# In the last group of a trunk layer's channel mixer, two more up channels by seven products, in turns with a pair; the group's weight sums on VectorE; one plain tile's low part by transfer

## The chip, the cores and the metric

One core of one Trainium2 chip runs the whole layer in one launch. The metric is the device time of one execution in microseconds (us). The kernel before has a median of 824.56 us of 3 runs (824.37 to 825.36). Engines: TensorE (PE, with its weight loads as PEld), VectorE (DVE), ScalarE (ACT), GpSimd (POOL), and SyncE (SP), which issues most loads.

## The reference

A decoder layer on 512 tokens of 1024 channels, all in float32. The part that matters here is the channel mixer at its end:

```python
u2 = _rmsnorm(h, norm2_g[l])
z = _causal_dwconv(u2 @ w_ffn_up[l], ffn_dw_w[l], ffn_dw_b[l])
h = h + (jax.nn.silu(z[..., :FFN_DIM]) * z[..., FFN_DIM:]) @ w_ffn_down[l]
```

`w_ffn_up` is 1024 x 5632, `w_ffn_down` 2816 x 1024, and the depthwise convolution has three taps. 2816 channels are 22 tiles of 128: "channel i" below means the value tile i and its gate tile 22 + i, two tiles of the up projection with 512 tokens each.

## The kernel before, in words

**Products.** TensorE multiplies in a rounded float32 form, so each weight and each activation is held as a high and a low part: ScalarE casts the high part, VectorE subtracts it from the original to get the low part, and each product is three matmuls (`mm3`, lines 448 to 450: high x low, low x high, high x high). A plain tile (`col_tile`) is 8 rows of 128 inputs x 3 matmuls of 512 columns. A weight tile of 128 x 1024 is loaded by SyncE into one of four `raw` buffers, then split (`split_weight`) into `whi` and `wlo`, four buffers each. `weight` hands out the next weight of a fixed list (`order`) and splits up to two ahead (`LOOK`). For some tiles (`ADDED`) the low part isn't VectorE's: ScalarE writes the negated rounded weight into `wlo`, and an accumulating transfer from GpSimd's queue adds the original from memory (lines 387 and 388).

**By seven.** A pair of tiles can be computed with Strassen and Winograd's seven products instead of eight: inputs halved (k), tokens halved (256), the two tiles being the output halves. `two_tiles` does so for channel i in four parts, named after the weight sums that they use: x1 (two products, 24 matmuls of 256 columns), x3 (24), x2 (24) and x4 (12). It uses three PSUM banks x, y, z, and two SBUF tiles c1 and c2 for the combined halves: ScalarE copies a bank's half out (line 1180), VectorE combines (line 1183). The sums of activations that the products need are made once, in the first group. The weight sums are made per channel on GpSimd (`two_sums`, line 327): from the two raw tiles "one" and "two" a third raw tile is filled, four additions of 128 x 512 per channel.

**Groups and units.** The 22 channels go in three groups of pairs (`GROUPS`; the last is (12, 14), (13, 15), (16, 18), (17, 19)). After each group the down projection of its pairs runs, also by seven products (`seven`), and adds to the residual `hres`. Within a group `up_plan` writes out the order: a *unit* is the second channel q of one pair by seven, in turns with the first channel f of the next pair as two plain tiles in pieces. In the last group the units are (14 with 13), (15 with 16), (18 with 17), and at the end channel 19 plain. The first unit starts with a piece of a plain tile ("opens"), and in every unit a piece of a plain tile stands between x2 and x4 of the pair.

**After a channel.** `value` and `gated` run the three taps: ScalarE the first with the bias (line 1499), VectorE two (line 1502) for each of the two tiles; then silu on ScalarE and the product on VectorE (line 1516). `first_of_pair` and `second_of_pair` make the sums for the down projection and split them (lines 1522 to 1544). `third_ahead` splits an x3 part one weight further ahead; the second channel's work is issued behind that low part and behind the last tap (`third`).

**Queues.** Each engine has one queue in order, and the order is settled when the program is built. VectorE's queue in the last group holds low parts (lines 356 and 390), combines, taps and the pair's sums; SyncE's the raw loads; GpSimd's the weight sums and then the accumulating transfers for the down projection (lines 300 and 317).

```python
seq = [x1, a1, x3, a2, x2, b1, x4, ("second", q), b2]
return seq + [("first", f)]
```

## Time and profile before

| | |
|---|---|
| median of 3 runs | 824.56 us (824.37 to 825.36) |
| the profiled execution | 825.34 us |
| its span, first to last instruction | 823.6 us |
| granted TensorE clock, mean | 0.999 |
| weight sums on GpSimd, L327 | 56 in the whole kernel, 12 of them from 700 to 750 us |
| last group, up projection | about 704.5 to 779 us |
| last group, down projection | about 779 to 814 us |

How to read it: the profile is of one execution. Busy time is the time that an engine had an instruction running; matmuls overlap, so TensorE's durations (0.28 us for 256 columns, 0.39 for 512) are longer than the distance from one start to the next, and that distance is the cost. The chain that ended last is followed back from the last instruction to what released it. A row of the view in order of time has the start in us from the span's begin, the duration, the engine, the line, the operation, the tiles written and read, the shape, how many in a row, and in brackets the idle time ahead with its releaser.

### The profile page before, as it was taken

Reading aid. Unit: us, or ns where it says so; the run is one execution under the profiler, and the core shown is the slowest. Engines: PE = TensorE matmul, PEld = TensorE weight load, DVE = VectorE, ACT = ScalarE, POOL = GpSimd, SP = SyncE. Lnnn points to the kernel's source line nnn. Section 1 sums busy time; section 2 is a strip of 40 time slices with the busy share of each in tenths; the row PEclk is TensorE's granted clock in tenths of the full one; section 3 lists DMA queues with packets and bytes.
Section 4 is the critical chain, followed back from the end, with each engine's and each line's share of the span. In section 5 each row is a group of like instructions: output and inputs, shape, how many; then the busy total and the mean of one; then the engine's idle time right before and its main releaser. Section 6 shows DMA issues by size and latency. Waiting matters only on the chain.

```text
span 823.6 us, 11562 instructions
## 1 busy us (share of the span) xinstructions
PE 814.8 (99%) x4323; PEld 703.4 (85%) x4323; DVE 719.2 (87%) x1165; ACT 450.0 (55%) x666; POOL 148.7 (18%) x133
## 2 busy tenths in 40 slices
PE   9999999999999999999999999999999999999996
PEld 7888888888888889999988898898889988899885
DVE  6689999998989699886788789979975999789996
ACT  6643447656654456684454546556435653456654
POOL 2000010001010213443001100230123301522012
PEclk9999999999999999999999999999999999999999
DMA  8355572553433103323647623145632456334662
GB/s 316 98 124 148 147 187 99 129 154 103 96 109 103 51 27 121 110 78 110 210 112 213 178 98 103 31 170 158 142 131 89 139 141 164 105 103 142 190 129 103
DMA packets 30616, 106.27 MB, mean 129 GB/s; under 512 B 3464, under 2 KB 3600, under 8 KB 30560
## 3 DMA queue, kind: packets, MB, share of 16 engines
q1 hardware_dynamic: 24784, 85.34, 30.3%
q0 software_dynamic: 5760, 20.19, 14.3%
q8 instruction: 34, 0.56, 0.3%
q14 instruction: 22, 0.18, 0.1%
q10 hardware_dynamic: 16, 0.00, 0.0%
HBM read 103.42 MB, written 2.10 MB: 128 GB/s over the span
## 4 chain that ended last, share of the span: by engine, by line
PE 98%; ACT 1%; DVE 0%; issue 0%; POOL 0%; POOLq 0%; ACTq 0%
PE mm L448 28%; PE mm L449 28%; PE mm L450 28%; PE mm L662 2%; PE ax L449 2%; PE ax L450 2%; PE ax L448 2%; PE ax L1069 1%; PE ax L1071 1%; PE ax L1050 1%; PE ax L1037 1%; PE mm L568 0%; PE ax L576 0%; PE ax L529 0%; PE ax L1035 0%; PE ax L1084 0%
## 5 line engine op out<-in xcount | busy, mean ns | idle before, releaser
L448 PE MATMUL mm<-uh,wlo 128*128 128x512 f32 (+1 forms) x672 | 244.5, 364 | 0.0
L449 PE MATMUL mm<-ul,whi 128*128 128x512 f32 (+1 forms) x672 | 242.3, 361 | 0.0
L450 PE MATMUL mm<-uh,whi 128*128 128x512 f32 (+1 forms) x672 | 242.1, 360 | 0.0
L450 PEld LDWEIGHTS mm<-uh,whi 128*128 128x128 f32 x672 | 126.8, 189 | 19.5
L448 PEld LDWEIGHTS mm<-uh,wlo 128*128 128x128 f32 x672 | 127.0, 189 | 18.8
L449 PEld LDWEIGHTS mm<-ul,whi 128*128 128x128 f32 x672 | 127.0, 189 | 18.6
L385 ACT CAST whi<-raw 128x1024 fp32r<-128x1024 f32 x86 | 89.5, 1046 | 58.2 <-PE mm L450 29.8
L356 DVE TENSOR_TENSOR wlo<-raw,whi 128x1024 fp32r<-128x1024 f32 x80 | 93.1, 1171 | 25.3 <-ACT whi L355 21.3
L327 POOL TENSOR_TENSOR raw<-raw,raw 128x512 f32<-128x512 f32 x42 | 67.5, 1608 | 212.3 <-DVE wlo L356 107.1
L390 DVE TENSOR_TENSOR wlo<-raw,whi 128x1024 fp32r<-128x1024 f32 x70 | 92.2, 1320 | 13.4 <-ACT whi L385 13.4
L355 ACT CAST whi<-raw 128x1024 fp32r<-128x1024 f32 x80 | 76.3, 957 | 36.1 <-PE mm L450 28.3
L788 DVE SCALAR_TENSOR_TENSOR c<-h,pp,c 128x255 f32<-128x255 f32 (+14 forms) x120 | 56.0, 467 | 3.2 <-ACT c L784 3.1
L788 DVE SCALAR_TENSOR_TENSOR c<-aside,btmp,c 128x255 f32<-128x255 f32 (+14 forms) x120 | 56.1, 467 | 0.0
L788 DVE SCALAR_TENSOR_TENSOR aside<-h,pp,aside 128x255 f32<-128x255 f32 (+6 forms) x112 | 52.3, 467 | 0.0
L355 ACT CAST whi<-kept 128x1024 fp32r<-128x1024 f32 (+1 forms) x32 | 31.7, 995 | 32.0 <-DVE kept L310 15.7
L1502 DVE SCALAR_TENSOR_TENSOR tmp<-mm,pp,tmp 128x511 f32<-128x511 f32 (+1 forms) x56 | 41.3, 740 | 4.0 <-ACT tmp L1499 3.9
L356 DVE TENSOR_TENSOR wlo<-kept,whi 128x1024 fp32r<-128x1024 f32 (+1 forms) x32 | 36.9, 1152 | 4.9 <-ACT whi L355 4.8
L1180 ACT COPY tmp<-mm 128x256 f32<-128x256 f32 x48 | 17.6, 367 | 33.8 <-PE mm L450 33.3
L1418 DVE TENSOR_TENSOR hres<-hres,mm 128x512 f32<-128x512 f32 (+1 forms) x49 | 32.2, 668 | 2.6 <-PE mm L450 2.4
L1499 ACT ACTIVATE tmp<-mm,pp 128x512 f32<-128x512 f32 x28 | 21.8, 777 | 19.1 <-PE mm L450 18.9
L387 ACT ACTIVATE wlo<-raw 128x1024 fp32r<-128x1024 f32 x16 | 16.9, 1059 | 22.1 <-PE mm L448 22.1
L1502 DVE SCALAR_TENSOR_TENSOR tmp<-tmp,pp,tmp 128x511 f32<-128x511 f32 (+1 forms) x32 | 27.7, 886 | 0.4
(351 smaller groups left out, 1777.5 us busy)
## 6 DMA issues: line engine op xcount, KB each, us to landing
raw<-in_w_up_dram SPq DMA_DIRECT2D x44, 512.0 KB, 4.2
raw<-in_w_glu_dram SPq DMA_DIRECT2D x16, 512.0 KB, 5.2
raw<-in_w_down_dram SPq DMA_DIRECT2D x15, 512.0 KB, 4.2
kept<-in_w_down_dram POOLq DMA_DIRECT2D x10, 512.0 KB, 5.7
raw<-in_w_v_dram SPq DMA_DIRECT2D x8, 512.0 KB, 5.8
raw<-in_w_qk_dram SPq DMA_DIRECT2D x8, 512.0 KB, 3.4
raw<-in_w_r_dram SPq DMA_DIRECT2D x8, 512.0 KB, 4.5
wlo<-in_w_r_dram POOLq DMA_DIRECT2D x8, 512.0 KB, 8.0
```

What stands on the lines that cost most here:

```text
L327: work = nc.gpsimd.tensor_tensor(out, x, y, ALU.add)
L355: nc.scalar.copy(hi, raw)
L356: two_low[:] = [nc.vector.tensor_tensor(lo, raw, hi.bitcast(F32), ALU.subtract)]
L385: nc.scalar.copy(hi, raw)
L390: pace[0] = nc.vector.tensor_tensor(lo, raw, hi.bitcast(F32), ALU.subtract)
L448: nc.tensor.matmul(acc, ll, rh, start=first, stop=False, **kw)
L449: nc.tensor.matmul(acc, lh, rl, start=False, stop=False, **kw)
L450: nc.tensor.matmul(acc, lh, rh, start=False, stop=last, **kw)
L788: nc.vector.scalar_tensor_tensor(out[:, j:], x[:, : half_t - j], w, out[:, j:], ALU.mult, ALU.add)
L1418: done = nc.vector.tensor_tensor(hres[t, n][:, c], hres[t, n][:, c], acc[:, c], op)
L1499: nc.scalar.activation(z, acc, AF.Identity, bias=pp[:, PP_FB + m : PP_FB + m + 1], scale=w[2])
L1502: nc.vector.scalar_tensor_tensor(z[:, s:], acc[:, : T - s], w[j], z[:, s:], ALU.mult, ALU.add)
```

## The change

- Channels 13 and 17 (`BOTH`) are computed by seven as well. Their units, (14 with 13) and (18 with 17), are now two channels by seven in turns: q x1, f x1, q x3, f x3, q x2, q x4, then q's second-of-pair work, f x2, f x4, then f's first-of-pair work. The unit (15 with 16) and the plain channel 19 stay.
- In these two units the weight sums are made in the two raw buffers themselves (`split_in_place`): no third raw tile; x3 is split in two halves, between which a sum is added.
- All weight sums of the last group are VectorE's (channel 15's by `two_sums` with its third tile).
- The low part of plain tile 38 (channel 16's gate) is made by a negation and an accumulating transfer, and that tile's matmuls go in another order: all that read the high part, then the eight that read the low part (`high_first`).
- Small things with it: bank y is taken when x3 begins (`lazy`), c1 of channels 13 and 17 has a buffer of its own, `next_ahead` splits the next weight whatever it is where a unit by turns ends its q, and a constant tile lies in another pool.

```diff
--- before.py
+++ after.py
@@ -32,6 +32,7 @@
 EPS = 1e-6
 O_PAIRS = ((0, 2), (1, 3), (4, 6), (5, 7))
 GROUPS = (((0, 2), (1, 3), (4, 6), (5, 7)), ((8, 10), (9, 11), (20, 21)), ((12, 14), (13, 15), (16, 18), (17, 19)))
+LAST = [q for _, q in GROUPS[-1]]
 AHEAD = 4
 
 MERGE = [("w_gb", 4, 5), ("w_gb", 6, 7), ("w_ga", 0, 1), ("w_ga", 2, 3), ("w_ga", 4, 5), ("w_ga", 6, 7)]
@@ -39,10 +40,13 @@
 BEHIND = [_HALVES[:3], _HALVES[3:6], _HALVES[6:9], _HALVES[9:]]
 BEHIND += [[("w_conv", m, half) for m in pair for half in range(2)] for pair in O_PAIRS[:2]]
 MERGE_REST = [("w_conv", m) for pair in O_PAIRS[2:] for m in pair]
+BOTH = (13, 17)
 LOOK = 2
 
 ADDED = {("w_glu", 2 * k) for k in range(2, KT)} | {("w_r", m) for m in range(KT)}
 ADDED |= {("w_v", KT // 2 + j) for j in (0, 1)}
+
+ADDED |= {("w_up", FT + 16)}
 RATE = 5.0
 WARM = (6, 1, 2, 2)
 MID = 4
@@ -134,7 +138,7 @@
     ones = cp.tile([P, P], F32, name="ones")
     mhalf = cp.tile([P, NT], F32, name="mhalf")
     shares = cp.tile([P, P], F32R, name="shares")
-    run64 = cp.tile([P, T], BF16, name="run64")
+    run64 = gp.tile([P, T], BF16, name="run64")
     keep = cp.tile([P, P], U8, name="keep")
     att = gp.tile([P, NT, P], F32, name="att")
 
@@ -153,6 +157,8 @@
         nc.gpsimd.memset(att, 0.0)
 
 
+    with_both = set(BOTH)
+
     def up_plan(gi):
 
 
@@ -164,6 +170,11 @@
 
         def unit(q, f, kind):
 
+            if f in BOTH:
+                with_both.add(q)
+                turns = ((q, "x1"), (f, "x1"), (q, "x3"), (f, "x3"), (q, "x2"), (q, "x4"), (f, "x2"), (f, "x4"))
+                seq = [("part", i, part) for i, part in turns]
+                return seq[:6] + [("second", q)] + seq[6:] + [("first", f)]
             a, b = f, FT + f
             x1, x3, x2, x4 = (("part", q, part) for part in ("x1", "x3", "x2", "x4"))
             a1, a2 = (("tile", a, ks) for ks in halves(4))
@@ -324,6 +335,9 @@
     def two_sums(name, p, q, part):
 
         def add(out, x, y):
+            if name == "w_up" and p in LAST:
+                nc.vector.tensor_tensor(out, x, y, ALU.add)
+                return
             work = nc.gpsimd.tensor_tensor(out, x, y, ALU.add)
             if name == "w_up":
                 tc.keep_in_program_order(work)
@@ -340,6 +354,29 @@
             one, _, three = pair_raws[name, p]
             add(three[:, left], three[:, right], one[:, right])
 
+    def split_in_place(hi, lo, name, p, q, part):
+
+        one, two = pair_raws[name, p]
+        left, right = slice(0, T), slice(T, D)
+
+        def add(x, y):
+            nc.vector.tensor_tensor(x, x, y, ALU.add)
+
+        def split(hi, lo, x):
+            nc.scalar.copy(hi, x)
+            two_low[:] = [nc.vector.tensor_tensor(lo, x, hi.bitcast(F32), ALU.subtract)]
+
+        if part == "x3":
+            split(hi[:, left], lo[:, left], one[:, left])
+            add(one[:, left], two[:, right])
+            add(two[:, left], two[:, right])
+            split(hi[:, right], lo[:, right], one[:, left])
+            add(one[:, right], one[:, left])
+            return
+        split(hi, lo, {"x1": one, "x2": two, "x4": one[:, right]}[part])
+        if part == "x1":
+            add(one[:, left], two[:, left])
+
     def split_weight(halves=False, between=None):
 
         if len(ready) < len(order):
@@ -348,10 +385,18 @@
             raw = raws[len(ready)]
             name, spec = order[len(ready)]
             if name in SEVEN or name == "two":
-                raw = operand(raw, *spec) if name in SEVEN else two_operand(*spec)
-                n = raw.shape[-1]
+                if name == "two" and spec[1] in with_both:
+                    n = T if spec[-1] == "x4" else D
+                else:
+                    raw = operand(raw, *spec) if name in SEVEN else two_operand(*spec)
+                    n = raw.shape[-1]
                 hi = wp.tile([P, D], F32R, tag="whi", name=nm("whi"), bufs=4)[:, :n]
                 lo = wp.tile([P, D], F32R, tag="wlo", name=nm("wlo"), bufs=4)[:, :n]
+                if name == "two" and spec[1] in with_both:
+                    split_in_place(hi, lo, *spec)
+                    ready.append((hi, lo))
+                    refill()
+                    return
                 nc.scalar.copy(hi, raw)
                 two_low[:] = [nc.vector.tensor_tensor(lo, raw, hi.bitcast(F32), ALU.subtract)]
                 with ExitStack() as order_of:
@@ -382,6 +427,13 @@
 
                 cols = [slice(j * T, (j + 1) * T) for j in range(2)]
                 return [[lambda c=c, part=part: part(c) for c in cols] for part in (high, low)]
+            if (name, spec) in ADDED and name == "w_up":
+                pace[0] = nc.scalar.mul(lo, raw, -1.0)
+                nc.gpsimd.dma_start(lo, a[name][spec], accum_op=ALU.add)
+                nc.scalar.copy(hi, raw)
+                ready.append((hi, lo))
+                refill()
+                return
             nc.scalar.copy(hi, raw)
             if (name, spec) in ADDED:
                 pace[0] = nc.scalar.mul(lo, raw, -1.0)
@@ -402,6 +454,14 @@
         if n == len(ready) < len(order) and order[n][0] == "two" and order[n][1][-1] == "x3":
             split_weight()
             return two_low[0]
+
+    def next_ahead():
+
+        n = used[0] + LOOK
+        if n == len(ready) < len(order):
+            two = order[n][0] == "two"
+            split_weight()
+            return two_low[0] if two else pace[0]
 
     two_low = []
 
@@ -460,6 +520,14 @@
             if k in at:
                 at[k]()
         return acc
+
+    def high_first(w, acts, acc, which):
+
+        every = [(k, 0, p) for k in range(KT) for p in (1, 0)] + [(k, 1, 0) for k in range(KT)]
+        for n in which:
+            k, of_w, of_act = every[n]
+            w_k = w[of_w][:, k * P : (k + 1) * P]
+            nc.tensor.matmul(acc, w_k, acts[k][of_act], start=n == 0, stop=n == len(every) - 1)
 
     def row_half(name, j0, n, acts, nk, done, tok_inner, middle=None):
 
@@ -1170,10 +1238,11 @@
 
     combined = []
 
-    def two_tiles(name, p, q, acts7, side_bank, at_once=False):
-
-        x, y, z = mm_bank(), side_bank(), side_bank()
-        c1, c2 = tmp(), tmp()
+    def two_tiles(name, p, q, acts7, side_bank, at_once=False, lazy=False, room=tmp):
+
+        x, z = mm_bank(), side_bank()
+        y = None if lazy else side_bank()
+        c1, c2 = room(), tmp()
         t1, t2 = slice(0, H), slice(H, T)
 
         def put(c, acc):
@@ -1192,6 +1261,7 @@
         combine(c1[:, t1], c1[:, t1], z[:, :H], ALU.add)
         yield
         w = weight("two", (name, p, q, "x3"))
+        y = y or side_bank()
         step(x, "n2", w, 1, False)
         put(c2[:, t1], x)
         step(y, "s1", w, 0, True)
@@ -1493,6 +1563,9 @@
     heap_scope.close()
     ffn_scope, fp = scoped("ffn", 1)
 
+    def seven_room():
+        return fp.tile([P, T], F32, tag="c1", name=nm("c1"), bufs=1)
+
     def ffn_conv(acc, m):
         z = tmp()
         w = [pp[:, PP_FW + m * FW + j : PP_FW + m * FW + j + 1] for j in range(FW)]
@@ -1656,17 +1729,21 @@
                 if 0 in rest[0]:
                     banks[i] = (weight("w_up", i), mm_bank())
                 wt, acc = banks[i]
-                col_tile(wt, acts2, acc, ks=rest[0])
+                if ("w_up", i) in ADDED:
+                    high_first(wt, acts2, acc, range(3 * rest[0].start, 3 * rest[0].stop))
+                else:
+                    col_tile(wt, acts2, acc, ks=rest[0])
                 if KT - 1 in rest[0] and i < FT:
                     values[i] = value(i, acc)
             if what == "part":
                 if rest[0] == "x1":
-                    units[i] = two_tiles("w_up", i, FT + i, lambda: up_acts, ax_bank)
+                    units[i] = two_tiles("w_up", i, FT + i, lambda: up_acts, ax_bank, lazy=True, room=seven_room if i in BOTH else tmp)
                 done = next(units[i])
                 if done:
                     values[i] = value(i, done[0])
                     banks[FT + i] = (None, done[1])
-                    third = [taps_at[0], third_ahead()]
+                    if i not in BOTH:
+                        third = [taps_at[0], next_ahead() if i in with_both else third_ahead()]
             if what == "first":
                 w = first_gated(i, values.pop(i), banks.pop(FT + i)[1])
                 if any(i in pair for pair in pairs):
```

## The prediction

> **What bounds the kernel now.** I read the page's busy line and its chain first, then the last group's stretches by engine, then TensorE's and VectorE's instructions in order of time.
>
> ```profile
> PE 814.8 (99%) x4323; PEld 703.4 (85%) x4323; DVE 719.2 (87%) x1165; ACT 450.0 (55%) x666; POOL 148.7 (18%) x133
> ...
> PE 98%; ACT 1%; DVE 0%; issue 0%; POOL 0%; POOLq 0%; ACTq 0%
> ```
>
> TensorE is busy for 99% of the span and is 98% of the chain that ended last. VectorE is next with 87%. So a matmul saved is time saved, as long as VectorE (which makes every weight's low part and every sum) still delivers in time. The change sits in the last group, so the next view is the busy time by stretch there: three units of a pair by seven beside a plain channel (704.5 to 767.8), the last plain channel 19 (to 779.0), then the down projection, cut at 804.2.
>
> ```profile
> 704.50:725.70 21.20, 21.20 (x135) 19.20 (x134) 12.87 (x15) 9.29 (x13) 9.39 (x6) 1.00 0.33 107
> 725.70:746.70 21.00, 21.00 (x134) 19.03 (x133) 20.82 (x27) 13.97 (x22) 6.91 (x4) 1.00 0.28 94
> 746.70:767.80 21.10, 21.10 (x134) 19.14 (x133) 19.01 (x28) 12.82 (x20) 1.74 (x1) 1.00 0.69 244
> 767.80:779.00 11.20, 11.20 (x51) 9.29 (x50) 11.16 (x18) 6.85 (x11) 1.73 (x2) 1.00 0.59 105
> 779.00:804.20 25.20, 25.20 (x113) 20.84 (x112) 24.80 (x35) 12.36 (x16) 3.44 (x4) 1.00 0.60 126
> 804.20:814.00 9.80, 9.80 (x45) 8.12 (x44) 7.28 (x12) 7.25 (x14) 2.84 (x4) 1.00 0.29 107
> ```
>
> The columns are stretch, length, then the busy time of PE, PEld, DVE, ACT, POOL, the granted clock (1.00 throughout) and the DMA share. TensorE has no gap in any of them. VectorE's idle time is 8.33 us in the first unit and then 0.18, 2.09, 0.04 and 0.40: 11.0 us up to 804.2, three quarters of it in the first unit, which has no taps of an earlier unit to do. From 725.7 on VectorE is all but full. That decides this case: the change buys TensorE time with VectorE work.
>
> **The change part by part.** *What TensorE saves.* The third unit shows both kinds of work; the stretches are cut at the steps' first matmuls, and the counts include two that reach over an edge.
>
> ```profile
> 746.69:749.57 2.88, 2.88 (x26) 1.00 0.53 182
> 749.57:752.99 3.42, 3.42 (x17) 1.00 0.46 153
> 738.33:739.76 1.43, 1.43 (x14) 1.00 0.84 246
> 746.69:767.71 21.02, 21.02 (x134) 1.00 0.69 244
> ```
>
> The first row is part x1, 24 matmuls of 256 columns (0.120 us each); the second is five of a plain tile's eight rows, 15 matmuls of 512 columns (0.228 each); the third is one step of 12 by 256 in the unit before (0.119). A plain channel (two tiles) is 48 x 0.228 = 10.94 us, a channel by seven 84 x 0.119 to 0.120 = 10.0 to 10.08; the whole unit, 21.02, is their sum. One channel saves 0.86 to 1.0 us, so 13 and 17 together **1.7 to 2.0; I take 1.9**. By the number of columns it would be 12.5%; the short matmuls cost 5% more a column, so 8.5% is left. The reordering of tile 38's matmuls (all that read its high part first) keeps their number: nothing.
>
> *What VectorE gains and loses.* Its instructions in order of time (start, duration, line, tiles); the difference of two starts is what one costs in a queue that is full.
>
> ```profile
> 701.37 2.25 DVE L390 TENSOR_TENSOR wlo<-raw,whi 128x1024 fp32r<-128x1024 f32 x1
> ...
> 717.95 1.23 DVE L356 TENSOR_TENSOR wlo<-raw,whi 128x1024 fp32r<-128x1024 f32 x1 [1.92 <-ACT whi L355]
> ...
> 735.68 0.68 DVE L1516 TENSOR_TENSOR w<-tmp,tmp 128x512 f32<-128x512 f32 x1
> 736.28 1.21 DVE L390 TENSOR_TENSOR wlo<-raw,whi 128x1024 fp32r<-128x1024 f32 x1
> 737.42 0.94 DVE L1522 TENSOR_TENSOR sl<-v,sh 128x768 fp32r<-128x768 f32 x1
> ...
> 739.88 0.40 DVE L1183 TENSOR_TENSOR tmp<-tmp,mm 128x256 f32<-128x256 f32 x1
> ...
> 743.68 2.32 DVE L390 TENSOR_TENSOR wlo<-raw,whi 128x1024 fp32r<-128x1024 f32 x1
> ...
> 747.06 3.10 DVE L1502 SCALAR_TENSOR_TENSOR tmp<-tmp,pp,tmp 128x511 f32<-128x511 f32 x3
> ...
> 767.66 2.19 DVE L1502 SCALAR_TENSOR_TENSOR tmp<-tmp,pp,tmp 128x511 f32<-128x511 f32 x3
> ```
>
> A 512-column sum costs 0.60 (735.68 to 736.28), a 1024-column low part 1.14; for a 256-column combine I take 0.33, its 0.40 less the overlap that the others show. Per new channel by seven: low parts 1.14 + 2 x 0.60 (x3 now in halves) + 1.14 + 0.60 = 4.1 instead of the plain 2 x 1.14 = 2.3, so +1.8; four weight sums, +2.4; three combines, +1.0. That is 5.2, and **10.4** for two. The sums of the pairs 14, 15 and 18 come over from GpSimd: 12 x 0.60 = **7.2**; two more x3 parts in halves, 0.1. Tile 38's low part goes to a transfer: **-1.1**. Together +16.6.
>
> Against that stands what GpSimd's sums cost VectorE now. The low parts at 701.37 and 743.68 took 2.25 and 2.32 instead of 1.21; three tap instructions at 747.06 took 3.10 where three such take 2.19. GpSimd had a sum running each time. Eight such places, the first at 701.37 and the last at 747.06, lost 6.3 us. With no sums left there, this goes: **-6.3**. Net +10.3 us of VectorE work up to 804.2, where 11.0 - 1.9 = 9.1 are free. **VectorE is short by 1.2 us** even if it never waits for anybody.
>
> [...]
>
> ```profile
> 716.81 3.52 POOL L327 TENSOR_TENSOR raw<-raw,raw 128x512 f32<-128x512 f32 x2 [5.24 <-DMA raw<-in_w_up_dram]
> 720.28 1.29 POOL L327 TENSOR_TENSOR raw<-raw 128x512 f32<-128x512 f32 x1
> ```
>
> A sum with VectorE idle took 1.29; the two ahead of it took 1.76 each, while VectorE's low part at 717.95 kept its 1.23: there GpSimd paid. [...]
>
> *Waits that are added.* In a unit by turns x4 follows x2 directly for both channels (a plain half tile stands between them now). x4's first matmul adds to the bank that the combine of x2's first step reads, so that combine has only x2's second step, 1.43 us, for cover. In the second unit that step ran from 738.33 to 739.76, and the combine ran at 739.88 (0.40): it would have been 0.5 us late. TensorE does everything in order, so all behind it waits. With four such places, two of them in the roomy first unit, that is 2 x 0.5 to 4 x 0.5 = 1.0 to 2.0 us. It is the same shortage seen where it bites, not a second one. **I take 1.6 us of new waits**, near the middle of 1.0 to 2.0 and above the ledger's 1.2, since VectorE also waits for the copies of the in-place sums. The ends for the range are 0 and the second rival's 4.4. Below nothing is excluded: TensorE waits nowhere in this group, so no wait can go away.
>
> *What is hidden.* ScalarE gets 2 x (1.5 casts of about 1.0 us + four copies of 0.3 to 0.4) + one negation, about 7 us beside 31.6 idle (74.5 less 42.9 busy) in the first four stretches. A unit by turns holds all four raw buffers; the next unit's loads go out as the first channel's raws come free, some 10 us before use, with 4.2 us to landing. If they came later, TensorE would wait a microsecond for each. GpSimd's queue only gets emptier: the accumulating transfers of the down projection stand behind fewer sums. The later choice of a bank, the tile that moved between pools and the extra tile are no instructions: nothing, and if a bank or buffer is missing, it shows as a TensorE wait.
>
> **Sum:** -1.9 + 1.6 = -0.3 us. The profiled execution took 825.34 (span 823.6); it would be 825.0. Its runs have a median of 824.56, 0.8 lower, so I predict **824.3 us**.
>
> **The rivals.** *Full gain.* The waits vanish because VectorE's order puts the combines and low parts first and lets the taps wait; they are due only in the down projection. For it: VectorE idles 2.09 us in the third unit now and has caught up there. Against it: the 1.2 us short. Then 824.56 - 1.9 = 822.7. [...]
>
> *VectorE becomes the bound (slower).* In place, x3 is a chain over two engines: ScalarE copies the left half, VectorE takes its low part and adds the next sum into the same buffer, ScalarE copies again, VectorE takes the right low part, which the step reads first.
>
> ```profile
> L355 ACT CAST whi<-raw 128x1024 fp32r<-128x1024 f32 x80 | 76.3, 957 | 36.1 <-PE mm L450 28.3
> ...
> L387 ACT ACTIVATE wlo<-raw 128x1024 fp32r<-128x1024 f32 x16 | 16.9, 1059 | 22.1 <-PE mm L448 22.1
> ...
> raw<-in_w_up_dram SPq DMA_DIRECT2D x44, 512.0 KB, 4.2
> ```
>
> A copy of half the 957 ns, say 0.6 us with its fixed part, and VectorE's 0.60 make 5 x 0.6 = 3.0 us, started two parts (5.76 us) ahead. So VectorE may be late by 1.4 us at each of the two crossings. The combine at 739.88 was some 1.4 late already, against the end of its step just past 738.33. With VectorE short, a lateness of about 3.6 at both crossings in the third unit, where taps of the unit before queue up too, gives 3.0 + 7.2 - 5.76 = 4.4 us of waits: -1.9 + 4.4 = +2.5, **827.1**. It turns slower than 0.2% from a lateness of 3.2 on (3.55 us of waits).
>
> *Tile 38's low part comes late (slower).* Its chain is load, negation, transfer.
>
> ```profile
> DMA to landing us min/median/max: 5.2/7.6/10.7
> ```
>
> These are the 16 transfers of this kind in the earlier stages. 4.2 + 1.06 + 7.6 = 12.9 us, up to 16.0; the raw buffer comes free with the sums of 15's x3, which run up to 3 us ahead of that part. From x3's start to the 17th matmul of tile 38, the first that reads the low part, TensorE has 2.88 + 2.05 + 2.86 + 2.74 + 1.43 + 0.9 = 12.9 us. So it is on time at the median and at worst 3 us late: -0.3 + 3 = +2.7, 827.3. [...]
>
> **How the numbers follow.** A measurement of this kernel can tell about 0.2% (1.65 us) from no change, so faster means under 822.9 and slower over 826.2. The forecast, with waits between 0.3 and 3.5 us, has 0.52 (own range 823.0 to 826.2); full gain 0.18; VectorE as the bound 0.22; the late low part 0.08. So faster 0.18, same 0.52, slower 0.30. The range goes from the full gain, 822.6, to the late cases, 827.3; beyond lie about 0.15 above and 0.04 below.
>
> **What would show it.** TensorE: 84 matmuls of 256 columns each for 13 and 17 at 0.119 to 0.120, and first gaps in the last group, before x4 or x3 of a unit by turns, most in the one with 18 and 17. VectorE: no low part of 2.2 us in the group, 20 sums of 0.68, under 1 us idle between 725 and 800. GpSimd: no sums there. Wrong would be: gaps in the first unit, gaps before tile 38's 17th matmul, VectorE with several microseconds of idle time while TensorE waits, or a plain channel that costs other than 10.9.

## The result and the profile after

The changed kernel takes 834.93 us (median of 5 runs, 832.83 to 836.58) against 824.75 us for the kernel before in the same session: a ratio of 1.0122, with an interval of 1.0109 to 1.0134. It is 10 us **slower**; the forecast was 824.3 us, its range 822.6 to 827.3. The profiled execution of the changed kernel took 832.83 us (span 831.1).

The busy line and the head of the chain that ended last, from the page of the changed kernel:

```profile
PE 815.4 (98%) x4395; PEld 706.1 (85%) x4395; DVE 728.0 (88%) x1198; ACT 457.1 (55%) x683; POOL 127.0 (15%) x122
...
PE 89%; DVE 4%; DMA 3%; issue 2%; ACT 1%; POOL 0%; POOLq 0%; ACTq 0%; DVEq 0%; SPq 0%
```

Before, TensorE was 98% of the chain. Now 8% of it is VectorE, transfers and ScalarE and 2% is "issue" (time in which the engine waited for nothing that the profile shows), though VectorE's busy share of the whole span rose by one point only. So look at the stretches: the first unit, the other units with the plain channel and the start of the down projection, its middle, and its last 9.8 us (columns as in the prediction's stretches).

```profile
703.80:724.30 20.50, 20.50 (x173) 20.46 (x171) 17.62 (x29) 12.49 (x20) 0.00 (x0) 1.00 0.21 78
724.30:785.20 60.90, 53.83 (x351) 48.38 (x350) 55.17 (x87) 37.10 (x59) 1.71 (x2) 1.00 0.45 139
785.20:811.70 26.50, 25.81 (x112) 20.59 (x111) 25.89 (x36) 12.76 (x17) 4.32 (x5) 1.00 0.67 139
811.70:821.50 9.80, 9.80 (x45) 8.12 (x44) 7.65 (x13) 7.24 (x14) 1.96 (x4) 1.00 0.29 109
```

The 168 matmuls of 256 columns from 703.97 to 724.05, as many as two channels by seven have, took 20.1 us, as forecast: the saving is there. (By the order in the program and the rows, the last twelve of them belong to channel 15's x1; 13's x4 runs behind the wait at 725.30.) In the second row TensorE has 7 us without work, in the third 0.7. These are its instructions that had to wait (start, duration, then in brackets the idle time ahead and what ended it):

```profile
725.30 0.39 PE L508 MATMUL mm<-uh,wlo 128*128 128x256 f32 x1 [0.73 <-DVE tmp L1252]
...
734.47 0.50 PE L530 MATMUL mm<-ul,whi 128*128 128x512 f32 x1 [0.71 <-ACT whi L433]
...
747.97 1.20 PE L530 MATMUL mm<-uh,wlo 128*128 128x512 f32 x4 [2.37 <-DMA wlo<-in_w_up_dram]
...
762.45 0.39 PE L508 MATMUL mm<-xq,wlo 128*128 128x256 f32 x1 [2.29 <-DVE wlo L367]
...
765.12 0.38 PE L508 MATMUL mm<-btmpq,wlo 128*128 128x256 f32 x1 [0.97 <-DVE wlo L367]
...
804.46 0.73 PE L508 MATMUL mm<-whi,sl 128*128 128x512 f32 x2 [0.47 <-DVE hres L1488]
805.41 0.74 PE L508 MATMUL mm<-whi,sl 128*128 128x512 f32 x2 [0.22 <-ACT whi L400]
```

In order: 13's x4 waits for its combine; tile 38 for its high part (0.7) and then for its low part's transfer (2.4); 17's x3, the chain in place (2.3), and its x2 (1.0); two sums of the down projection. Taken from start to start, less the usual distance, the seven are 0.89 + 0.86 + 2.54 + 2.45 + 1.13 + 0.64 + 0.49 = 9.0 us (each 0.15 to 0.27 more than its time in brackets), and with some smaller ones behind them **9.9**. From the first unit's first matmul to the first 256-column matmul at the end of the down projection it was 117.5 us (703.97 to 821.45) instead of 109.3 (704.67 to 813.95): 8.2 more, which is, to 0.1, the 9.9 of waits less the 1.8 saved (2 x 10.94 - 20.08). The other four runs took 1.6 to 3.8 us longer than the profiled one, at a mean granted clock of 0.993 to 0.995 where this one had 0.999; the last section comes back to that.

**The ledger that counts.** VectorE's busy and idle time, from the first unit to the start of the last 9.8 us, from the stretches of each kernel (before's are in the prediction; the others come from the same view of each kernel, three of them shown). "More work" is against the kernel before.

| kernel | length | VectorE busy | more work | idle, first unit | idle, behind it |
|---|---|---|---|---|---|
| before | 99.7 | 88.7 | | 8.3 | 2.7 |
| changed | 107.9 | 98.7 | +10.0 | 2.9 | 6.3 |
| changed, no transfer | 107.0 | 99.1 | +10.5 | 3.6 | 4.3 |
| sums alone | 99.7 | 89.3 | +0.7 | 6.8 | 3.6 |
| sums and 4.2 us | 101.1 | 93.5 | +4.9 | 6.6 | 1.0 |
| sums and 8.4 us | 104.5 | 97.4 | +8.7 | 6.6 | 0.5 |
| changed, no transfer, 9.2 us less | 99.5 | 91.0 | +2.4 | 2.6 | 5.9 |

VectorE's work grew by 10.0 us; the prediction's ledger had 10.3. What was wrong is the other side. Of its 11.0 us of idle time VectorE still has 9.2, and behind the first unit it has more than before.

### The profile page after: what moved, and what is told of

It is laid out like the page before. It is cut to its first block, busy times and chain, and to the rows that moved or that the text cites. A ratio compares the mean times of both kernels' runs of the same rounds, so it can differ in the third digit from the quotient of the medians.

```text
span 831.1 us, 11741 instructions
## 1 busy us (share of the span) xinstructions
PE 815.4 (98%) x4395; PEld 706.1 (85%) x4395; DVE 728.0 (88%) x1198; ACT 457.1 (55%) x683; POOL 127.0 (15%) x122
## 4 chain that ended last, share of the span: by engine, by line
PE 89%; DVE 4%; DMA 3%; issue 2%; ACT 1%; POOL 0%; POOLq 0%; ACTq 0%; DVEq 0%; SPq 0%
PE mm L508 25%; PE mm L509 25%; PE mm L510 25%; PE mm L730 3%; PE ax L508 2%; PE ax L510 2%; PE ax L509 2%; DMA wlo<-in_w_up_dram 1%; DMA raw<-in_w_up_dram 1%; DVE tmp L1575 1%; PE ax L1137 1%; DVE wlo L401 1%; DMA kept<-in_w_down_dram 1%; PE ax L1139 1%; PE ax L1118 1%
## 5 line engine op out<-in xcount | busy, mean ns | idle before, releaser
L508 PE MATMUL mm<-uh,wlo 128*128 128x512 f32 (+1 forms) x648 | 233.6, 360 | 0.7 <-DVE tmp L1252 0.7
L509 PE MATMUL mm<-ul,whi 128*128 128x512 f32 (+1 forms) x648 | 231.2, 357 | 0.0
L510 PE MATMUL mm<-uh,whi 128*128 128x512 f32 (+1 forms) x648 | 231.1, 357 | 0.0
L508 PEld LDWEIGHTS mm<-uh,wlo 128*128 128x128 f32 x648 | 122.5, 189 | 18.4 <-DVE tmp L1252 0.9
L510 PEld LDWEIGHTS mm<-uh,whi 128*128 128x128 f32 x648 | 122.4, 189 | 17.9
L509 PEld LDWEIGHTS mm<-ul,whi 128*128 128x128 f32 x648 | 122.5, 189 | 17.3
L437 ACT CAST whi<-raw 128x1024 fp32r<-128x1024 f32 x81 | 84.5, 1046 | 55.9 <-PE mm L510 30.2
L401 DVE TENSOR_TENSOR wlo<-raw,whi 128x1024 fp32r<-128x1024 f32 x72 | 83.7, 1169 | 21.4 <-ACT whi L400 18.7
L442 DVE TENSOR_TENSOR wlo<-raw,whi 128x1024 fp32r<-128x1024 f32 x65 | 82.5, 1272 | 13.4 <-ACT whi L437 13.4
L400 ACT CAST whi<-raw 128x1024 fp32r<-128x1024 f32 x72 | 68.6, 959 | 32.3 <-PE mm L510 24.8
L341 POOL TENSOR_TENSOR raw<-raw,raw 128x512 f32<-128x512 f32 x33 | 51.5, 1562 | 178.9 <-DVE wlo L401 99.8
L400 ACT CAST whi<-kept 128x1024 fp32r<-128x1024 f32 (+1 forms) x32 | 31.7, 995 | 38.7 <-DVE kept L321 20.1
L1575 DVE SCALAR_TENSOR_TENSOR tmp<-mm,pp,tmp 128x511 f32<-128x511 f32 (+1 forms) x48 | 35.4, 741 | 4.0 <-ACT tmp L1572 3.9
```

Source lines behind the costliest of these rows:

```text
L341: work = nc.gpsimd.tensor_tensor(out, x, y, ALU.add)
L400: nc.scalar.copy(hi, raw)
L401: two_low[:] = [nc.vector.tensor_tensor(lo, raw, hi.bitcast(F32), ALU.subtract)]
L437: nc.scalar.copy(hi, raw)
L442: pace[0] = nc.vector.tensor_tensor(lo, raw, hi.bitcast(F32), ALU.subtract)
L508: nc.tensor.matmul(acc, ll, rh, start=first, stop=False, **kw)
```

## The experiments

Two theories. **Order:** the waits come from chains between engines that the change made, each with its place (the combine ahead of x4, 17's x3 in place, tile 38's transfer); put those right and the waits go. **Amount:** VectorE has more work than it can place where TensorE needs it, whatever the chains; a place put right only moves the wait to the next. In the expectations from experiment 9 on, theory A is amount and B is order; the first ones call order "chains". The kernels are the changed one with the edit shown; in all of them the kernel before ran on the same chip (medians 824.6 to 824.9).

**1. Without the transfer** (VectorE makes tile 38's low part again).

```diff
-ADDED |= {("w_up", FT + 16)}
```

> The changed kernel, with tile 38's low part by VectorE again and its matmuls in the old order. Theory (chains): the waits of TensorE in the changed kernel (9.9 us in its profile) come from separate chains that are late, each at its own place; the transfer's is 2.5 us ahead of tile 38's low part and 0.9 ahead of its first matmul. Both go, the others stay: 4.0 to 4.8 us faster than the 834.9 of the changed kernel with fewer gaps, about 829 to 831, although VectorE has 1.1 us more to do. Rival (amount): TensorE waits because VectorE has too much to do in all; then 1.1 us more for VectorE means at least as much waiting elsewhere, 834 to 836.

Measured: 832.86 us, ratio 1.0069 to 1.0114. That is between the two theories' ranges. The two waits at tile 38 go, and the others grow, from 2.29 to 2.90 and from 0.73 to 1.28; a new one of 0.6 stands at 15's x3:

```profile
725.74 0.39 PE L507 MATMUL mm<-uh,wlo 128*128 128x256 f32 x1 [1.28 <-DVE tmp L1251]
...
760.81 0.39 PE L507 MATMUL mm<-xq,wlo 128*128 128x256 f32 x1 [2.90 <-DVE wlo L366]
```

The medians differ by 2.1 us, but the intervals meet (1.0069 to 1.0114 here, 1.0109 to 1.0134 before) and the two profiled executions, both at a clock of 0.998 to 0.999, differ by 0.8 (832.83 and 832.02). So the late transfer explains some 1 to 2 of the 10 us, not more.

**2. Channel 13 alone by seven** (17 plain, transfer kept).

```diff
-BOTH = (13, 17)
+BOTH = (13,)
```

> The changed kernel with channel 13 alone added by seven, 17 plain; the transfer and the sums on VectorE stay. Chains: the gap ahead of 13's x4 (about 1 us) and the transfer's (3.4) stay, the 3.6 us in the unit of 18 and 17 go; matmuls save 0.95. About 824.75 - 0.95 + 1 + 3.4 = 828.2, up to 830 if the clock dips. Amount: VectorE has 5.2 us less than in the changed kernel and so room; gaps nearly all gone, 824 to 825.5.

Measured: 827.87 us, 1.0023 to 1.0046. Waits of 0.8 at 700.6, 0.6 at 734 and 1.1 at 746 (the transfer again). This is near what chains gave (828.2) and far from what amount gave (824 to 825.5): with 5.2 us less VectorE work the waits at tile 38 stay.

**3. Channel 17 alone by seven** (13 plain, transfer kept).

```diff
-BOTH = (13, 17)
+BOTH = (17,)
```

> The changed kernel with channel 17 alone added by seven, 13 plain. Chains: transfer 3.4 and the unit of 18 and 17 with 3.6 to 3.8 us of gaps stay, tail about 1; saves 0.95. About 824.75 - 0.95 + 3.4 + 3.7 + 1 = 832, or less for the transfer's part if its raw tile comes earlier. Amount: as with 13 alone, 824 to 825.5.

Measured: 829.84 us, 1.0040 to 1.0070. The time lies between the two theories (832, and 824 to 825.5). The transfer is on time; 17's x3 chain waits 2.0. One channel costs 3, the other 5, both 10: the parts add up to a little less than the whole.

**4. The sums alone** (both channels plain, no transfer, the last group's weight sums on VectorE).

```diff
-BOTH = (13, 17)
+BOTH = ()
-ADDED |= {("w_up", FT + 16)}
```

> The kernel before with the last group's weight sums on VectorE and nothing else of the change but its small things (later bank, pool of the constant tile). Ledger of the prediction: 12 sums cost VectorE 7.2 us and give back 6.3 that GpSimd's took from it: no change, 824.3 to 825.3. Rival: the sums in VectorE's queue wait for loads and hold up what is behind them; then 1 us or more slower, 825.8 or over, with gaps where a pair's raw tiles land late.

Measured: 824.75 us, 0.9987 to 1.0006: no difference. VectorE's stretches (first unit, up to channel 19's end, down projection to the last 9.8 us):

```profile
704.20:725.40 21.20, 21.20 (x135) 19.20 (x134) 14.38 (x20) 9.19 (x13) 0.00 (x0) 1.00 0.28 92
725.40:778.70 53.30, 53.30 (x315) 47.49 (x314) 50.15 (x76) 33.64 (x51) 1.71 (x2) 1.00 0.51 155
778.70:803.90 25.20, 25.20 (x112) 20.85 (x112) 24.80 (x35) 12.38 (x16) 3.44 (x4) 1.00 0.59 126
```

Eleven of the twelve sums lie in these stretches, 6.6 us at 0.60 each, and VectorE's busy time rose by 0.7 only: most of what GpSimd's sums had cost it, 6.3 in the prediction, is won back. That step held.

**5. 17's chain in place ahead of the pair's work** (17 alone; the weight whose chain waited is split right behind 15's last part).

```diff
-BOTH = (13, 17)
+BOTH = (17,)
...
                         third = [taps_at[0], next_ahead() if i in with_both else third_ahead()]
+                        if gi == len(GROUPS) - 1 and i == 15:
+                            split_weight()
+                            third.append(two_low[0])
```

> As the kernel with channel 17 alone by seven (829.84), with the same instructions; only 17's x3 part is split one step earlier, so that its copies, low parts and in-place sums stand ahead of channel 15's and 16's work for the down projection in ScalarE's and VectorE's queues. Theory (order of a chain): the gaps of 2.1 and 0.4 us ahead of 17's x3 and x2 go, and with them the half-clock window that followed; about 826, with 1.2 us of gaps in the down projection left. Rival (amount of VectorE work): the amount is the same, the waiting moves elsewhere, 829 to 831.

Measured: 829.14 us, 1.0036 to 1.0066, against 829.84 without the edit. The wait at 17's x3 is gone, and its like stands 31 us later, in the down projection:

```profile
790.82 0.51 PE L509 MATMUL ax<-wlo,ah 128*128 128x512 f32 x1 [1.99 <-DVE wlo L401]
```

The order was put right and the wait moved. That speaks for amount.

**6. Channel 13 alone, no transfer.**

```diff
-BOTH = (13, 17)
+BOTH = (13,)
-ADDED |= {("w_up", FT + 16)}
```

> The changed kernel with channel 13 alone by seven and tile 38's low part by VectorE. With channel 13 alone and the transfer the time was 827.87, with gaps of 0.6 and 1.1 us at tile 38 and 0.8 at 700 us. Theory (chains): the two at tile 38 go, the matmuls' 0.95 stays: 824.75 - 0.95 + 0.3 to 1.1 = 824.1 to 825. Amount: VectorE gets 1.1 us more, the waits stay: 827.5 to 829.

Measured: 825.96 us, 1.0007 to 1.0024. Again between the two (824.1 to 825, and 827.5 to 829): the waits at tile 38 go, one of 0.57 stands at 15's x3, and even in the roomy unit one channel by seven doesn't gain.

**7. The transfer alone** (both channels plain, the sums back on GpSimd).

```diff
-LAST = [q for _, q in GROUPS[-1]]
+LAST = []
-BOTH = (13, 17)
+BOTH = ()
```

> The kernel before with tile 38's low part by transfer alone (and the small things). If the transfer was late because its raw tile came late, behind a unit by turns that holds all four raw buffers, it is on time here: 824.3 to 825.3. If the transfer as such takes too long for its place (8 to 10 us against 7.6 at the median in the earlier stages), there is a gap ahead of tile 38's 17th matmul and 1 to 2.5 us more, 826 to 827.

Measured: 824.92 us, 0.9993 to 1.0011, and no wait. The transfer is late only behind 13's unit by turns. There tile 38's load goes out at 728.05 (changed kernel) and 727.95 (experiment 2), without it at 724.50 (experiment 3) and 723.74 (here), though this landing took 8.3 us, as in experiment 2.

**8. Both places in order** (both channels, no transfer; 13's last combines ahead of the next unit's weight work, which at the end of 14 is no longer split ahead, and 17's chain early as in 5).

```diff
-ADDED |= {("w_up", FT + 16)}
...
-        w = weight("two", (name, p, q, "x2"))
+        w = weight("two", (name, p, q, "x2"), 1 if name == "w_up" and p == 13 else LOOK)
...
+        if name == "w_up" and p == 13:
+            with tc.issue_after(combined[0].ins):
+                prefetch(LOOK)
...
-                        third = [taps_at[0], next_ahead() if i in with_both else third_ahead()]
+                        third = [taps_at[0], next_ahead() if i in with_both and i != 14 else third_ahead()]
+                        if gi == len(GROUPS) - 1 and i == 15:
+                            split_weight()
+                            third.append(two_low[0])
```

> Both channels by seven, tile 38's low part by VectorE (that kernel took 832.86), the same instructions with two pieces moved in the queues: 13's combine ahead of 15's sums, and 17's x3 chain ahead of 15's and 16's work for the down projection. Theory (order): the gaps of 1.45, 3.05 and 1.1 us go, those of 0.8 ahead of 15's x3, 0.6 and 1.2 in the down projection may stay: 824.75 - 1.9 + 2.5 = 825.4, at best 823.5. Rival (amount): VectorE's work is the same, so is the time: 831 to 834.

Measured: 833.22 us, 1.0087 to 1.0114, where 832.86 was without the order. Neither of the two chains is waited for any more. Where 13's x4 waited 1.28, TensorE now waits 0.61 for a low part, one wait of 3.0 stands at the plain tile behind, for a low part that was put back, and two of 1.3 and 1.0 in the down projection:

```profile
731.55 0.50 PE L507 MATMUL mm<-uh,wlo 128*128 128x512 f32 x1 [3.01 <-DVE wlo L441]
```

Order as the whole cause falls here.

**9 and 10. VectorE's work by itself.** The next two kernels have none of the new chains: both channels plain, as in 4, and the product of gate and up is done twice or three times in the last group, with the same result.

```diff
-BOTH = (13, 17)
+BOTH = ()
-ADDED |= {("w_up", FT + 16)}
...
-        nc.vector.tensor_tensor(out, za, zb, ALU.mult)
+        for _ in range(3 if last[0] else 1):
+            nc.vector.tensor_tensor(out, za, zb, ALU.mult)
...
+        last[0] = gi == len(GROUPS) - 1
```

> The version with plain channels 13 and 17 and the weight sums on VectorE (it took the time of the kernel before, 824.75 us), with the product of gate and up done twice in each of the last group's seven units of VectorE work: 7 x 0.60 = 4.2 us more for VectorE, spread over the group, nothing more for any other engine and no new chain between engines. Theory A (VectorE's amount of work, with idle time that can't be used): 4.2 us takes about half of the 11 us that were idle, so waits of 0 to 1.5 us, 824.8 to 826.3. Theory B (the waits come from the chains of the steps by turns, whatever VectorE's amount): no new wait, 824.6 to 825.0.

Measured: 826.08 us, 1.0006 to 1.0024 (a range of 2 in the diff). The first 4.2 us cost 1.3.

> The same with the product done three times: 14 x 0.60 = 8.4 us more for VectorE, about what the ledger gave for the two channels by seven with their sums already counted. Theory A: TensorE waits for VectorE by 3 to 8 us, 828 to 833, although every unit is built as in the kernel before. Theory B: still under 826.3, since 8.4 us is less than the 11 us idle.

Measured: 829.82 us, 1.0044 to 1.0072. The second 4.2 us cost 3.7. Its stretches:

```profile
704.30:725.50 21.20, 21.20 (x135) 19.20 (x134) 14.56 (x20) 9.20 (x13) 0.00 (x0) 1.00 0.28 94
725.50:778.80 53.30, 53.30 (x315) 47.38 (x314) 52.81 (x79) 32.25 (x49) 1.71 (x2) 1.00 0.50 151
778.80:808.80 30.00, 26.69 (x113) 20.45 (x113) 30.00 (x45) 13.65 (x18) 3.44 (x4) 1.00 0.54 113
808.80:818.60 9.80, 9.80 (x45) 8.12 (x44) 7.64 (x13) 7.25 (x14) 1.96 (x4) 1.00 0.26 97
```

This is the cleanest picture of the case. In the third row VectorE is busy for 30.00 of 30.00 us, and all of TensorE's waits are there, at a place that nobody touched. The first of them (row below) is for a weight's low part, which the extra products only keep back in the queue: they lengthen no chain that leads to it. In the first row VectorE is idle for 6.6 of 21.2 us, 6.8 without the extra work. That idle time couldn't be used: the products belong to channels that aren't computed yet. Three rows of VectorE from that unit and its end say why it stands still:

```profile
787.91 0.50 PE L508 MATMUL mm<-wlo,sh 128*128 128x512 f32 x1 [1.66 <-DVE wlo L400]
...
720.03 0.42 DVE L1251 TENSOR_TENSOR tmp<-tmp,mm 128x256 f32<-128x256 f32 x1 [1.06 <-PE mm L509]
721.46 0.42 DVE L1251 TENSOR_TENSOR tmp<-ax,tmp 128x256 f32<-128x256 f32 x1 [1.01 <-PE ax L509]
...
725.64 1.23 DVE L400 TENSOR_TENSOR wlo<-raw,whi 128x1024 fp32r<-128x1024 f32 x1 [1.86 <-PE mm L509]
```

It waits for TensorE: for results to combine, and for a `wlo` buffer to be read out.

**11. The changed kernel with less for VectorE** (both channels, no transfer; the last group's third tap is left out, a part of the computation).

```diff
-ADDED |= {("w_up", FT + 16)}
...
-        for j, s in ((1, 1), (0, 2)):
+        for j, s in ((1, 1), (0, 2))[: 1 if last[0] else 2]:
```

> Both channels by seven, tile 38's low part on VectorE, and the last group's third tap (of a depthwise kernel of three) left out, so part of the computation is missing: 14 x 0.66 = 9.2 us less for VectorE, nothing else changed. Theory A: the waits in front of x4, of 17's x3 and in the down projection go down to 0 to 2 us in all, and the saving of TensorE shows: 822.7 to 825.0. Theory B: the waits in front of x4 and of 17's x3 stay at 3 us or more and the time is over 826.

Measured: 824.66 us, 0.9989 to 1.0007: 8.2 less than with the tap. In the profile the waits are 2.0 us where they were 9 to 10, and none is left in the down projection:

```profile
724.59 0.39 PE L507 MATMUL mm<-uh,wlo 128*128 128x256 f32 x1 [0.52 <-DVE tmp L1251]
```

The others are 0.65 ahead of 17's x3, 0.27 ahead of its x2 and some of 0.1. So with VectorE relieved the chains cost about 2.0 us, as much as the two channels save; the other 8 are there only with the amount. That isn't the amount's price by itself, since a tap that is left out also makes every chain behind it start earlier.

**12. Channel 13 alone, with transfers that can be early** (tiles 16 and 41 in the place of 38; VectorE does 2.3 us less).

```diff
-BOTH = (13, 17)
+BOTH = (13,)
-ADDED |= {("w_up", FT + 16)}
+ADDED |= {("w_up", 16), ("w_up", FT + 19)}
```

> Channel 13 alone by seven, with two plain low parts of tiles whose raw buffer is free early (16 and 41) taken by transfer in the place of tile 38's: VectorE loses 2 x 1.14 = 2.3 us against the version with 13 alone and no transfer (825.96 us, with waits of about 1.3 us). Theory A: the waits vanish and the 0.9 to 1.0 us of saving is left: 823.7 to 824.6. Theory B, or a transfer that lands late: 825.5 to 828.

Measured: 825.09 us (824.15 to 825.55), 0.9990 to 1.0008: 0.9 less than without the transfers, which is the direction of theory A, but outside its range (823.7 to 824.6) and not the saving of TensorE. One wait of 0.36 (0.52 from start to start) is left, and the runs stand in two clusters, five from 824.15 to 824.63 and six from 825.09 to 825.55. The interval says no difference.

**13. The same with 13's combines ahead of the next unit's weight work**, as in 8.

```diff
+        w = weight("two", (name, p, q, "x2"), 1 if name == "w_up" and p == 13 else LOOK)
...
+        if name == "w_up" and p == 13:
+            with tc.issue_after(combined[0].ins):
+                prefetch(LOOK)
...
-                        third = [taps_at[0], next_ahead() if i in with_both else third_ahead()]
+                        third = [taps_at[0], next_ahead() if i in with_both and i != 14 else third_ahead()]
```

> The run before last's kernel (13 alone by seven, low parts of 16 and 41 by transfer, 825.09 us) with 13's last combines put ahead of the next unit's weight work in VectorE's order. Its one wait left in the last group is 0.5 us in front of 13's x4. If order is what is left of it (theory B's part, once VectorE has room): the wait goes, 824.2 to 824.7, the first version under the kernel before. If the wait only moves to another place (theory A still binding): 824.9 to 825.6.

Measured: 825.95 us, 1.0008 to 1.0026. The hoped-for gain fell, and by more than my other case: the wait stayed, now for the weight that the combine was put ahead of, and tile 16's transfer, started later, is late too.

```profile
725.37 0.39 PE L508 MATMUL mm<-uh,wlo 128*128 128x256 f32 x1 [0.61 <-DVE wlo L401]
...
733.43 0.73 PE L530 MATMUL mm<-uh,wlo 128*128 128x512 f32 x2 [1.27 <-DMA wlo<-in_w_up_dram]
```

**14. Both channels, with the transfers of tiles 16 and 41.**

```diff
-ADDED |= {("w_up", FT + 16)}
+ADDED |= {("w_up", 16), ("w_up", FT + 19)}
```

> Both channels by seven, the whole computation, with the two low parts of tiles 16 and 41 by transfer and tile 38's on VectorE: 2 x 1.14 = 2.3 us less for VectorE than the version without any transfer (832.86 us). Theory A, each microsecond of VectorE work past its usable idle time costs one: 829.8 to 831.3, with the waits lower by about 2.3. Theory B: 832.0 to 833.5. Transfers that land late would show as waits on a DMA.

Measured: 831.63 us (830.35 to 832.25), 1.0066 to 1.0097. 2.3 us less work saved 1.2, between the two theories and above A's range: one for one is too simple here, since one of the transfers landed 0.74 late and 17's x3 still waits 2.4. No version beat the kernel before.

## Why the prediction was wrong, step by step

- **What bounds the kernel** (TensorE, with VectorE all but full behind the first unit): right.
- **TensorE saves 1.9:** right, 1.8 by the measured 168 matmuls (20.08 us, two channels at 10.04 each). It is 9.9 of waits that hide it.
- **VectorE's work, +16.6 less 6.3 of what GpSimd's sums had cost:** right, +10.3 forecast and +10.0 measured in the profiles; experiment 4 shows the exchange of the sums by itself at no cost (824.75 us, VectorE's busy time up by 0.7). (One of the eight places, 701.37, and one of the twelve sums lie ahead of 704.5, where the ledger begins; 1.0 and 0.6 us, which nearly cancel.)
- **"11.0 - 1.9 = 9.1 are free": the step that failed.** I had written that three quarters of the idle time lie in the first unit, and then put it in one sum with work that falls due later. Experiment 10 shows it: 8 us more of VectorE work behind the first unit, and that unit's 6.6 us stay idle while VectorE has no idle time left where the taps and the down projection's operands meet. Behind the first unit only 2.7 of the 11.0 us lay; experiment 9's first 4.2 us used up most of what was there (3.6 to 1.0 in the table) and cost 1.3. In the changed kernel 4.75 of the 10.0 us went to the first unit (12.87 to 17.62), where they cost little. The other 5.3, and the 1.0 that TensorE needs less time for 17, met those 2.7: short by 3.6, not by 1.2. Experiment 10 gives the same size: there 7.0 us more work than before behind the first unit cost 4.8 of time, so the 6.3 here would cost an estimated 4.1 by their amount alone. The rest of the 9.9 is the next step.
- **"I take 1.6 us of new waits … it is the same shortage seen where it bites, not a second one":** mis-sized, 9.9 measured, and it was a second one. The chains cost 2.0 with VectorE relieved (experiment 11), and the shortage comes on top. That 2.0 is near my 1.6 is luck in part: I had counted four combines ahead of x4, and only 13's was waited for (0.7 of the 2.0); the others are at 17's x3 and x2. And VectorE's idle time behind the first unit rose from 2.7 to 6.3 instead of being used up. As a sum that holds by itself, 5.3 more work + 1.0 less TensorE time + 3.6 more idle = 9.9 of waits; it doesn't say why VectorE stood idle. The rows of the changed kernel do: of nine gaps of 0.27 to 1.22 us, 6.2 in all, 3.2 us go back to a product of TensorE, directly or by way of ScalarE, so there the two engines wait for each other. The other 2.9 go back to a load that landed late, most by way of ScalarE's casts, which waited for it:

```profile
744.27 1.05 ACT L366 CAST whi<-raw 128x1024 fp32r<-128x1024 f32 x1 [1.79 <-DMA raw<-in_w_up_dram]
...
768.84 1.05 ACT L437 CAST whi<-raw 128x1024 fp32r<-128x1024 f32 x1 [3.76 <-DMA raw<-in_w_up_dram]
...
791.49 1.05 ACT L400 CAST whi<-kept 128x1024 fp32r<-128x1024 f32 x1 [2.12 <-DMA kept<-in_w_down_dram]
```

The prediction had held the loads to be in time. No run here makes them earlier, so what their lateness cost TensorE stays open.
- **The rival "VectorE becomes the bound"** had the mechanism and the place (17's x3 in place, 2.3 of idle, and 1.0 at its x2), with 2.5 us against a measured 10. I had priced one chain in one unit, and the waits of a full queue went on down to the sums at 804.
- **The rival "tile 38's low part comes late"** held as well: its share is 1 to 2 us (experiment 1). The load went out at 728.05, the cast came at 733.37, the negation at 736.57, the transfer at 738.03. The landing took 9.9 us, inside the 5.2 to 10.7 quoted, with four other loads of 512 KB issued from 735.46 on; when the load goes out 4 us earlier nothing waits (experiment 7). I gave these two rivals a chance each as if one excluded the other; they came together.
- **"Wrong would be: gaps in the first unit, gaps before tile 38's 17th matmul, VectorE with several microseconds of idle time while TensorE waits":** all three happened (0.7 at the first unit's end, 2.4 at the tile, 6.3 of idle behind the first unit).

What of the 8 us is pure amount and what is chains and loads made late by a full queue isn't settled: experiment 10 prices the amount at some 4, experiment 14 took 2.3 us of work away and got 1.2 back, experiment 11 took 9.2 and got 8.2.

The rows of VectorE at the first of the waits show the two at work in one place. 13's combine (724.84) was ready to run when its product ended, some 721.3, and stands behind the next unit's sums (L339), a low part and three taps, in the order settled at build time; the first of these sums had itself waited 0.95 for a load.

```profile
719.90 0.69 DVE L339 TENSOR_TENSOR raw<-raw,raw 128x512 f32<-128x512 f32 x1 [0.95 <-DMA raw<-in_w_up_dram]
720.51 1.22 DVE L401 TENSOR_TENSOR wlo<-raw,whi 128x1024 fp32r<-128x1024 f32 x1
721.65 0.68 DVE L339 TENSOR_TENSOR raw<-raw,raw 128x512 f32<-128x512 f32 x1
722.25 0.74 DVE L1575 SCALAR_TENSOR_TENSOR tmp<-tmp,pp,tmp 128x511 f32<-128x511 f32 x1
722.91 0.68 DVE L339 TENSOR_TENSOR raw<-raw 128x512 f32<-128x512 f32 x1
723.51 1.40 DVE L1575 SCALAR_TENSOR_TENSOR tmp<-tmp,pp,tmp 128x510 f32<-128x510 f32 x2
724.84 0.41 DVE L1252 TENSOR_TENSOR tmp<-tmp,mm 128x256 f32<-128x256 f32 x1
```

## What to carry to other kernels

Idle time of an engine isn't a sum to draw on: count it stretch by stretch, from the point where the new work exists to the point where it is due, and let only that part pay. Where an engine has no idle time left in a stretch, as behind the first unit in experiment 9 (1.0 of 79.9 us), price further work there at nearly its full length (3.7 of 4.2 us here), add the chains between engines as a second term, and look whether putting one chain in order only moves the wait to the next place, as it did in experiments 5 and 8. To find out which of the two it is, give a kernel without the new chains the same amount of extra work: two such runs said more here than those that changed the order or the transfers.

## What the runs showed of the hardware

Some waits of TensorE cost more behind them. In experiment 3, the 256-column products of 17's x3 start 0.12 us apart behind the wait of 1.96 us; 1.3 us later they stand 0.21 apart and take 0.41 instead of 0.28, for 3.4 us, and then it is over:

```profile
759.38 0.39 PE L508 MATMUL mm<-xq,wlo 128*128 128x256 f32 x1 [1.96 <-DVE wlo L367]
759.72 0.28 PE L510 MATMUL mm<-xq,whi 128*128 128x256 f32 x1
...
761.82 0.42 PE L509 MATMUL mm<-usq,whi 128*128 128x256 f32 x1
...
763.11 0.41 PE L509 MATMUL mm<-usq,whi 128*128 128x256 f32 x1
...
764.25 0.28 PE L509 MATMUL ax<-xq,whi 128*128 128x256 f32 x1
```

The granted clock, sixth of the values behind the length of each stretch, says the same:

```profile
759.30:760.60 1.30, 1.22 (x10) 1.22 (x11) 1.30 (x4) 0.00 (x0) 0.00 (x0) 1.00 0.00 0
760.60:764.00 3.40, 3.26 (x16) 2.97 (x16) 2.53 (x3) 0.89 (x2) 0.00 (x0) 0.51 0.42 145
764.00:767.40 3.40, 3.40 (x30) 3.40 (x30) 2.02 (x4) 1.26 (x2) 0.00 (x0) 0.99 0.91 327
```

By an estimate from these rows, half of 3.4 us, 1.7 us at most are lost there. Such a stretch came behind waits of 1.99 us (experiment 5, products of 512 columns 0.43 apart instead of 0.23), 3.01 (experiment 8, a mean clock of 0.64 from 731.40 to 736.00) and 2.41 (experiment 14, products of 256 columns 0.21 apart) as well, and not behind the 2.37 and 2.29 of the changed kernel's own profile (clock 1.00 from 747.50 to 751.40 and from 762.00 to 766.00) nor the 2.90 of experiment 1 (1.00 from 724.20 to 784.00). So in these profiles the length of a wait doesn't decide it by itself; what does, they don't settle.

Such slow stretches are a likely reason why runs of one kernel with such waits spread: one costs an estimated 1.7 us at most, and the changed kernel's runs at a mean clock of 0.993 to 0.995 lie 1.6 to 3.8 us above its profiled one (0.999), so some 2 of the 10.2 us between the medians may be clock. That last step is argued from the clocks, since only one of these runs was profiled.
